# The second product of both MLPs by one level of Strassen's scheme: seven block products in place of eight

## The chip, the cores and the metric

The kernel runs on one core of one Trainium2 chip. Its metric is the device time of one execution in microseconds (us); three runs before the change gave a median of 1163.3 us (1161.93 to 1166.11). A core has TensorE (PE, matrix products; PEld is its weight load), VectorE (DVE), ScalarE (ACT), GpSimd (Pool) and SyncE (SP), whose queue issues all loads and stores here.

## The reference, cut to what matters

Two residual layers over 512 tokens of width 1024. Layer 0 mixes tokens by gating groups and stick-breaking attention, layer 1 by an mLSTM; each is followed by the same MLP with 4096 inner columns.

```python
def _sqrelu_mlp(h, w1, w2):
    return jnp.square(jax.nn.relu(h @ w1)) @ w2

def reference(x, ...):
    for layer in range(DEPTH):            # DEPTH = 2
        h = _rmsnorm(x, mix_norm_g[layer])
        ...                               # even mixer, odd mixer
        h = _rmsnorm(x, mlp_norm_g[layer])
        x = x + _sqrelu_mlp(h, mlp_w1[layer], mlp_w2[layer])
    return x
```

## The kernel before

Everything lies transposed: the residual `xs` (xres) is eight tiles of 128 features by 512 tokens. All large products are made in float32r, and each operand is split into a rounded part and the rest (`hi`, `lo`); `mm3` then makes three products, hi x hi, hi x lo and lo x hi (L228, L229, L230). The operand of the current part is `xhi`, `xlo`.

The weights come in half units of 128x1024 float32 (512 KB), in the order of their use. `w_fetch` loads one on SP's queue into `wr` (two buffers), ACT copies its rounded part to `wh` (L168) and DVE subtracts to `wl` (L169); `wh` and `wl` have six buffers each. `w_take(n)` hands out the next n units and fetches six further ones ahead (LA).

An MLP (`mlp`, called once after each mixer) runs over 8 groups of 512 inner columns. The first product of a group makes 4 tiles, each in a PSUM bank of tag A or C with 24 products of 128x512; DVE takes it out with the ReLU and the norm's factor (`r`, L561), ACT squares it (`s`, L563), ACT and DVE split it (`hh`, L224, and `hl`, L225). The second product makes the 8 feature tiles `d` one after another, each in a bank of tag B (three of them) with 12 products of 128x512, and DVE adds the bank to `xs` (L578). In the last group of the last MLP each tile is stored at once (L580), the eighth in two halves.

In the last group of the first MLP `enter` goes along: as soon as a tile of `xs` is final, ACT and DVE make the next part's `xhi` and `xlo` (L220, L221), ACT squares it (L276), and the squares are added up (L277), on Pool, the last on DVE. `norm_cols` makes the factor of each token from the sum, and the odd mixer's first values (`proj_v`) use it when their banks are taken out.

The program is written in this order and a scheduler puts each engine's instructions into the order in which they are issued; every engine then works through its own queue in order.

## Time and profile before

| | |
|---|---|
| median of 3 runs | 1163.3 us (1161.93 to 1166.11) |
| span of the profiled execution, first to last instruction | 1157.4 us |
| what lies around the span, median less span | 5.9 us |
| PE busy | 1136.7 us, 98% |
| PE weight loads | 927.1 us, 80% |
| DVE busy | 635.3 us, 55% |
| ACT busy | 448.2 us, 39% |
| Pool busy | 159.9 us, 14% |
| loads from memory | 102 MB, 26.9% of the 16 DMA engines' time |

The profiled execution has a span but no time of its own; its time is taken as the span and the 5.9 us around it. Matmuls are pipelined and their ends are modelled: a single one of 128x512 is shown as 0.39 us long while the next starts 0.23 us after it. So the distance from start to start is what a product costs, not the length of its row. Busy times of DVE and ACT can be read as they stand; back to back, their rows overlap a little.

### The profile page before, as it was taken

The page shows a single profiled execution, that of the slowest core. Times are in us where ns is not written, and L with a number is a line of the kernel's source. Part 1 is how long each engine was busy: PE and PEld are TensorE (multiplying, and loading weights), DVE is VectorE, ACT ScalarE, POOL GpSimd, SP SyncE. Part 2 cuts the span into 40 slices and gives each one's busy share as a digit, 9 for nine tenths or more (in the row PEclk, how much of TensorE's full clock was granted, in tenths as well). Part 3 has the DMA queues.
Part 4 walks back from the last instruction along what each step waited for, and adds up shares of the span by engine and source line. Part 5 has one row for each costly group of instructions (what it writes and reads, how often), then busy time and mean ns, then how long its engine had stood idle before and what let it go on. Part 6 is the DMA issues. An engine that isn't in the chain of part 4 may idle for free.

```text
span 1157.4 us, 13308 instructions
## 1 busy us (share of the span) xinstructions
PE 1136.7 (98%) x5220; PEld 927.1 (80%) x5220; DVE 635.3 (55%) x916; ACT 448.2 (39%) x704; POOL 159.9 (14%) x152
## 2 busy tenths in 40 slices
PE   8999989999999999999999999999999999999998
PEld 5788777878888888888898888887888888888886
DVE  7753698644354353453667665878452453443542
ACT  5443686542142241241555443435331331331330
POOL 7327554510000000000020010013000000000000
PEclk8999999999999999999999999999999999999999
DMA  6323210242241241331332203312231331321421
GB/s 230 106 73 110 76 35 1 92 130 73 73 146 50 96 127 55 110 114 66 113 110 73 92 26 102 110 52 94 83 117 52 112 110 52 130 99 48 146 73 73
DMA packets 33486, 105.01 MB, mean 91 GB/s; under 512 B 3600, under 2 KB 8208, under 8 KB 33424
## 3 DMA queue, kind: packets, MB, share of 16 engines
q1 hardware_dynamic: 33424, 104.17, 26.9%
q8 instruction: 41, 0.67, 0.2%
q14 instruction: 21, 0.17, 0.1%
HBM read 102.06 MB, written 2.10 MB: 90 GB/s over the span
## 4 chain that ended last, share of the span: by engine, by line
PE 90%; DVE 5%; ACT 1%; POOL 1%; DMA 1%; issue 1%; SPq 0%; DVEq 0%; ACTq 0%; POOLq 0%
PE psB L228 11%; PE psB L229 11%; PE psB L230 11%; PE psA L230 11%; PE psA L228 11%; PE psA L229 11%; PE psC L228 5%; PE psC L230 5%; PE psC L229 5%; PE psO L228 2%; PE psO L230 2%; PE psO L229 2%; DVE m L475 2%; DMA xres<-xT 1%; DVE xlo L225 0%
## 5 line engine op out<-in xcount | busy, mean ns | idle before, releaser
L168 ACT ACTIVATE wh<-wr 128x1024 fp32r<-128x1024 f32 (+1 forms) x188 | 197.7, 1060 | 456.8 <-PE psB L229 285.4
L169 DVE TENSOR_TENSOR wl<-wr,wh 128x1024 fp32r<-128x1024 f32 x172 | 214.2, 1254 | 151.1 <-ACT wh L168 145.9
L578 DVE TENSOR_TENSOR xres<-psB,xres 128x512 f32<-128x512 f32 x129 | 85.9, 684 | 249.9 <-PE psB L230 249.9
L229 PE MATMUL psB<-hl,wh 128*128 128x512 f32 x512 | 199.2, 394 | 0.0
L230 PE MATMUL psB<-hh,wl 128*128 128x512 f32 x512 | 199.0, 394 | 0.0
L228 PE MATMUL psB<-hh,wh 128*128 128x512 f32 x512 | 194.2, 394 | 0.0
L228 PEld LDWEIGHTS psB<-hh,wh 128*128 128x128 f32 x512 | 96.1, 188 | 23.1 <-DVE xres L578 0.6
L229 PE MATMUL psA<-xlo,wh 128*128 128x512 f32 x292 | 114.4, 392 | 0.0
L229 PEld LDWEIGHTS psB<-hl,wh 128*128 128x128 f32 x512 | 96.2, 188 | 22.6
L230 PEld LDWEIGHTS psB<-hh,wl 128*128 128x128 f32 x512 | 96.1, 188 | 22.5
L228 PE MATMUL psA<-xhi,wh 128*128 128x512 f32 x288 | 112.5, 392 | 0.6 <-ACT wh L168 0.6
L230 PE MATMUL psA<-xhi,wl 128*128 128x512 f32 x288 | 112.9, 392 | 0.0
L228 PE MATMUL psC<-xhi,wh 128*128 128x512 f32 x256 | 101.0, 395 | 0.0
L230 PE MATMUL psC<-xhi,wl 128*128 128x512 f32 x256 | 100.8, 394 | 0.0
L229 PE MATMUL psC<-xlo,wh 128*128 128x512 f32 x256 | 100.6, 393 | 0.0
L228 PE MATMUL psA<-wh,xhi 128*128 128x512 f32 (+2 forms) x232 | 88.5, 383 | 2.0 <-ACT wh L168 1.9
L229 PE MATMUL psA<-wl,xhi 128*128 128x512 f32 (+2 forms) x232 | 88.6, 382 | 0.9 <-DVE wl L169 0.9
L230 PE MATMUL psA<-wh,xlo 128*128 128x512 f32 (+2 forms) x232 | 88.0, 381 | 0.7 <-DVE xlo L225 0.7
L277 POOL TENSOR_TENSOR ssq<-ssq,sq 128x512 f32<-128x512 f32 x18 | 27.6, 1536 | 362.4 <-ACT sq L276 362.4
L228 PEld LDWEIGHTS psA<-xhi,wh 128*128 128x128 f32 x288 | 54.1, 188 | 13.0 <-ACT wh L168 1.0
L229 PEld LDWEIGHTS psA<-xlo,wh 128*128 128x128 f32 x292 | 54.9, 188 | 12.0
L230 PEld LDWEIGHTS psA<-xhi,wl 128*128 128x128 f32 x288 | 54.1, 188 | 11.9
(334 smaller groups left out, 1728.4 us busy)
## 6 DMA issues: line engine op xcount, KB each, us to landing
wr<-wall SPq DMA_DIRECT2D x186, 512.0 KB, 3.5
out<-xres SPq DMA_DIRECT2D x7, 256.0 KB, 2.0
wr<-wv SPq DMA_DIRECT2D x2, 528.0 KB, 4.0
xres<-xT SPq DMA_DIRECT2D x4, 256.0 KB, 6.4
xres<-xT SPq DMA_DIRECT2D x2, 512.0 KB, 9.0
lngb<-lngb SPq DMA_DIRECT2D x1, 512.0 KB, 5.5
sgr<-sgw SPq DMA_DIRECT2D x1, 512.0 KB, 6.3
out<-xres SPq DMA_DIRECT2D x2, 128.0 KB, 1.7
```

Of the source, the lines that this page charges most:

```text
L168: act.activation(hi[:, :n], raw[:, :n], AF.Copy)
L169: (gp if i in POOL_LO else dve).tensor_tensor(lo[:, :n], raw[:, :n], f(hi[:, :n]), op=ALU.subtract)
L228: pe.matmul(out, lhsT=lh, rhs=rh, start=first, stop=False)
L229: pe.matmul(out, lhsT=lh, rhs=rl, start=False, stop=False)
L230: pe.matmul(out, lhsT=ll, rhs=rh, start=False, stop=last)
L277: (dve if i == KT - 1 else gp).tensor_tensor(ssq, ssq, j, op=ALU.add)
L475: dve.tensor_tensor_scan(m[:, ::-1], m[:, ::-1], ones.to_broadcast([P, n]), 1.0, op0=ALU.mult, op1=ALU.mult)
L578: dve.tensor_tensor(xs[:, d, cq], b[:, cq], xs[:, d, cq], op=ALU.add)
```

## The change

The second product is made as 2x2 blocks by Strassen's scheme (in the variant with fifteen sums) with seven block products. The blocks split the inner columns (a group is now 1024 columns, two blocks of 512; four groups in place of eight), the output features (0 to 511 and 512 to 1023) and the tokens (two halves of 256, `H`). Half `s` of a group covers 256 features of each feature block.

- Weights: `stream` takes the place of `w_fetch`. For a half it loads the four blocks b11, b12, b22, b21 (128x1024 each, the same bytes as before) into `wq` tiles and makes four sums of them on DVE (`w_sum`, L196), into `wq` tiles too (seven buffers for both). Seven units are split on ACT (L189) and DVE (L190) in place of four. `wh` and `wl` have five buffers instead of six.
- Activations: `operands` makes from the squared tiles (`h`) the seven right-hand operands of `PROD`, four of them by differences on DVE (L644, L654), each split on ACT (L636) and DVE (L640, L638), in two portions `q` of half a group.
- Products: `prod` runs 24 products of 128x256 for a block product, two output tiles in the two halves of a bank. a11 and a12 share a bank, n3 and -a22, n1 and n4; the banks are added from PSUM to `xs` and to `accm`, a tile of 128x1024, seven times a half (L680).
- `accm` collects what four groups give to three output blocks. It is added to them (three adds of 128x512) behind the last group's half, so the four tiles of a half become final together; `enter` or the stores (L694) follow then.
- The pool `vp` of the odd mixer, with the load of `gbias` and the memsets of `v_tiles`, is opened after the first MLP instead of before it.

```diff
+NG = 4
+F_ORDER = (0, 1, 4, 5, 2, 3, 6, 7)
...
     def mlp(l):
         w1, w2 = f("mlp_w1")[l], f("mlp_w2")[l]
-        for g in range(8):
-            for ft in range(4):
-                stat_cols(w1, (4 * g + ft) * P)
-            rows(w2[g * 512:(g + 1) * 512])
+        for g in range(NG):
+            for ft in F_ORDER:
+                stat_cols(w1, (8 * g + ft) * P)
+            for s in range(2):
+                for kb, nb in ((0, 0), (0, 1), (1, 1), (1, 0)):
+                    r0, c0 = g * 1024 + kb * 512, nb * 512 + s * 256
+                    hu.append(w2[r0:r0 + 512, c0:c0 + 256].reshape(4, P, 256).transpose(1, 0, 2).reshape(P, 1024))
...
+    NRAW = 7
+    NSPL = 5
...
+    def w_sum(a, b):
+        cnt[0] += 1
+        t = q_tile(f"wq_s{cnt[0]}")
+        dve.tensor_tensor(t, a, b, op=ALU.add)
+        return t
+
+    def stream():
...
+            if m is not None and (i - m) % 16 >= 8:
+                b11 = w_load(i, True)
+                w_split(b11, i)
+                yield
+                b12 = w_load(i + 1, True)
+                b22 = w_load(i + 2, True)
+                w_split(w_sum(b12, b22), i)
+                yield
+                a = w_sum(b11, b12)
+                w_split(a, i)
+                yield
+                b21 = w_load(i + 3, True)
+                w_split(b21, i)
+                yield
+                c = w_sum(a, b22)
+                w_split(w_sum(c, b21), i)
+                yield
+                w_split(b22, i)
+                yield
+                w_split(c, i)
+                yield
+                i += 4
...
+    PROD = ("a11", "n3", "n1", "a12", "-a22", "n4", "s2")
+    H = T // 2
...
+                put("a11", a11)
+                diff("n3", a21, a11)
+                n1 = diff("n1", a21, a22)
+                put("a12", a12)
+                put("-a22", a22, True)
+                s2 = mp.tile([P, 2, H], F32, name=f"s2_{cnt[0]}", tag="ad", bufs=3)
+                dve.tensor_tensor(s2, a11, n1, op=ALU.subtract)
+                diff("n4", a12, s2)
+                put("s2", s2)
...
+                        for dd in range(2):
+                            o = bk[key][:, dd * H:(dd + 1) * H]
+                            for k in range(4):
...
+                                pe.matmul(o, lhsT=lh, rhs=rh, start=first, stop=False, skip_group_check=True)
+                                pe.matmul(o, lhsT=lh, rhs=rl, start=False, stop=False, skip_group_check=True)
+                                pe.matmul(o, lhsT=ll, rhs=rh, start=False, stop=fin, skip_group_check=True)
...
+                    add(mv, prod("a11", "a", True, False), ALU.subtract)
+                    add(blk(1, 1, s), prod("n3", "b", True, False))
+                    add(blk(1, 1, s), prod("n1", "c", True, False))
+                    add(blk(0, 0, s), prod("a12", "a", False, True))
+                    add(blk(0, 1, s), prod("-a22", "b", False, True), ALU.subtract)
+                    add(blk(1, 0, s), prod("n4", "c", False, True))
+                    add(mv, prod("s2", "d", True, True, "O"))
+                    if g == NG - 1:
+                        add(blk(1, 0, s), mv)
+                        add(blk(1, 1, s), mv)
+                        add(blk(0, 1, s), mv, ALU.subtract)
+                        for d in (2 * s, 2 * s + 1, 4 + 2 * s, 5 + 2 * s):
+                            if last:
+                                nc.sync.dma_start(out=O["out"][d], in_=xs[:, d, :])
+                            yield d
```

Where the instructions stand now. On DVE, where the first product of a group in the first MLP ends and the second begins, before the change:

```order
L561 SCALAR_TENSOR_TENSOR r_3186<-psC_3161,rrow 128x512
L169 TENSOR_TENSOR wl_3157<-wr_3155,wh_3156 128x1024
L225 TENSOR_TENSOR hl_3191<-s_3188,hh_3190 128x512
L578 TENSOR_TENSOR xres<-psB_3218,xres 128x512
L578 TENSOR_TENSOR xres<-psB_3232,xres 128x512
```

The same place on DVE in the changed kernel's second group (n_206 and s_206 are the differences n1 and s2; psB_3315 is the bank of a11, psB_3341 that of n3):

```order
L710 SCALAR_TENSOR_TENSOR r_3246<-psC_3221,rrow 128x512
L190 TENSOR_TENSOR wl_3186<-wq_s_3183,wh_3185 128x1024
L644 TENSOR_TENSOR n_206_3255<-h_3111,h_3180 128x512
L640 TENSOR_TENSOR a12l_2940<-h_3180,a12h_2939 128x512
L196 TENSOR_TENSOR wq_s_3291<-wq_3275,wq_3281 128x1024
L680 TENSOR_TENSOR accm<-accm,psB_3315 128x512
L638 SCALAR_TENSOR_TENSOR -a22l_2942<-h_3180,-a22h_2941 128x512
L654 TENSOR_TENSOR s_206_3263<-h_3111,n_206_3255 128x512
L190 TENSOR_TENSOR wl_3218<-wq_3053,wh_3217 128x1024
L640 TENSOR_TENSOR n1l_2938<-n_206_3255,n1h_2937 128x512
L680 TENSOR_TENSOR xres<-xres,psB_3341 128x2x256
```

Between the evacuation of the last first-product and the add of the first bank stood one split and one `hl`; now two splits, a sum and the first operand steps stand among the adds, and n1's second part comes tenth.

On PE at the same place, before the change (bank of the last first-product, then the first tile of the second product):

```order
L230 MATMUL psC_3161<-xhi,wl_2910 128x512
L228 MATMUL psB_3218<-hh_3073,wh_2915 128x512
L229 MATMUL psB_3218<-hl_3074,wh_2915 128x512
L230 MATMUL psB_3218<-hh_3073,wl_2916 128x512
L228 MATMUL psB_3218<-hh_3112,wh_2921 128x512
```

And on PE in the changed kernel, two block products later (a11 and n3, 24 rows each, stand ahead of this piece):

```order
L676 MATMUL psB_3341<-n3h_2935,wl_3058 128x256
L674 MATMUL psB_3367<-n1h_2937,wh_3114 128x256
L675 MATMUL psB_3367<-n1l_2938,wh_3114 128x256
L676 MATMUL psB_3367<-n1h_2937,wl_3115 128x256
L674 MATMUL psB_3367<-n1h_2937,wh_3114 128x256
L675 MATMUL psB_3367<-n1l_2938,wh_3114 128x256
L676 MATMUL psB_3367<-n1h_2937,wl_3115 128x256
L674 MATMUL psB_3367<-n1h_2937,wh_3114 128x256
L674 MATMUL psB_3315<-a12h_2939,wh_3148 128x256
L675 MATMUL psB_3315<-a12l_2940,wh_3148 128x256
```

The scheduler breaks n1 off after seven products (the first six use the older portion of its operand), runs the whole of a12 and two products of s2, and takes up n1 again behind them.

At the end of the kernel DVE's last rows were

```order
L578 TENSOR_TENSOR xres<-psB_8908,xres 128x512
L578 TENSOR_TENSOR xres<-psB_8923,xres 128x512
L578 TENSOR_TENSOR xres<-psB_8938,xres 128x256 x2
```

and are now, with all eight stores of 128x512 behind the weights' loads in SP's queue, four of them for these last three adds:

```order
L680 TENSOR_TENSOR xres<-xres,psB_10403 128x2x256
L680 TENSOR_TENSOR accm<-accm,psO_10504 128x512
L680 TENSOR_TENSOR xres<-xres,accm 128x2x256 x3
```

Where the first MLP ends, the same adds stand among the splits of the odd mixer's weights, with the second parts of its operand (L283) and the sum of squares (L339) behind them:

```order
L680 TENSOR_TENSOR accm<-accm,psO_5268 128x512
L190 TENSOR_TENSOR wl_5100<-wr_5097,wh_5099 128x1024
L680 TENSOR_TENSOR xres<-xres,accm 128x2x256 x3
L190 TENSOR_TENSOR wl_5106<-wr_5103,wh_5105 128x1024
L283 SCALAR_TENSOR_TENSOR xlo<-xres,par,xhi 128x512 x4
L339 TENSOR_TENSOR ssq<-ssq,sq_7_5314 128x512
```

Before, the adds of the tiles came one by one, each followed by its own `xlo`.

## Rows read from the trace of the kernel before

**Rows 1.** The page's table of engines: busy us, share of the span, instructions.

```profile
span 1157.4 us, 13308 instructions
PE 1136.7 (98%) x5220; PEld 927.1 (80%) x5220; DVE 635.3 (55%) x916; ACT 448.2 (39%) x704; POOL 159.9 (14%) x152
```

**Rows 2.** The page's chain that ended last, its shares of the span by engine.

```profile
PE 90%; DVE 5%; ACT 1%; POOL 1%; DMA 1%; issue 1%; SPq 0%; DVEq 0%; ACTq 0%; POOLq 0%
```

**Rows 3.** Who waited for whom, over the whole span: us in total, times, longest. The last two are PE's own waits for weights.

```profile
ACT wh L168 <- PE psB L229: 285.4, 16, 23.1
DVE wl L169 <- ACT wh L168: 145.9, 108, 10.1
...
PE psA L228 <- ACT wh L168: 2.5, 2, 1.9
...
PE psA L229 <- DVE wl L169: 0.9, 1, 0.9
```

**Rows 4.** Stretches of the span: us, then busy us (instructions) of PE, PEld, DVE, ACT, Pool, then the granted clock, the DMA share and GB/s. The first lies inside the first MLP, the second around its end.

```profile
480.00:530.00 50.00, 50.00 (x219) 40.63 (x218) 21.80 (x27) 13.15 (x16) 0.00 (x0) 1.00 0.26 86
...
580.00:630.00 50.00, 49.45 (x326) 44.10 (x324) 34.99 (x58) 28.46 (x40) 5.80 (x8) 1.00 0.32 106
```

**Rows 5.** The chain that ended last in order of time (start, us, what): the same three products in three groups that follow one another in the first MLP.

```profile
436.06 0.70 PE psB L228 x3
480.48 0.70 PE psB L228 x3
524.85 0.69 PE psB L228 x3
```

**Rows 6.** PE's instructions in order of time in the odd mixer (start, us): the first and the last of 39 products of 128x256 in a row.

```profile
604.99 0.28 PE L229 MATMUL psA<-wl,xhi 128*128 128x256 f32 x1
...
609.50 0.28 PE L228 MATMUL psA<-wh,xhi 128*128 128x256 f32 x1
```

**Rows 7.** PE's weight loads in order of time (start, us) in a run of such products: two neighbours, and the last of 18.

```profile
599.88 0.19 PEld L229 LDWEIGHTS psA<-wl,xhi 128*128 128x128 f32 x1
600.00 0.19 PEld L230 LDWEIGHTS psA<-wh,xlo 128*128 128x128 f32 x1
...
601.89 0.19 PEld L228 LDWEIGHTS psA<-wh,xhi 128*128 128x128 f32 x1
```

**Rows 8.** Groups of instructions of DVE and ACT in 330 to 580 us, inside the first MLP: busy us, mean ns of one, idle before them and its releaser.

```profile
L169 DVE TENSOR_TENSOR wl<-wr,wh 128x1024 fp32r<-128x1024 f32 x43 | 52.2, 1224 | 40.5 <-ACT wh L168 40.3
L578 DVE TENSOR_TENSOR xres<-psB,xres 128x512 f32<-128x512 f32 x46 | 30.7, 688 | 87.2 <-PE psB L230 87.2
L225 DVE TENSOR_TENSOR hl<-s,hh 128x512 fp32r<-128x512 f32 x24 | 16.6, 691 | 1.3 <-ACT hh L224 1.2
...
L168 ACT ACTIVATE wh<-wr 128x1024 fp32r<-128x1024 f32 x43 | 45.1, 1059 | 142.9 <-PE psB L229 108.2 <-DMA wr<-wall 33.5 <-PE psA L230 1.1
L224 ACT ACTIVATE hh<-s 128x512 fp32r<-128x512 f32 x23 | 14.5, 629 | 0.6
```

**Rows 9.** DVE in order of time in the first MLP (start, us of the merged row): three adds and two splits back to back.

```profile
481.91 1.89 DVE L578 TENSOR_TENSOR xres<-psB,xres 128x512 f32<-128x512 f32 x3 [3.83 <-PE psB L230]
...
499.98 2.36 DVE L169 TENSOR_TENSOR wl<-wr,wh 128x1024 fp32r<-128x1024 f32 x2 [0.86 <-ACT wh L168]
```

**Rows 10.** The page's DMA issues: count, KB each, median us from issue to landing.

```profile
wr<-wall SPq DMA_DIRECT2D x186, 512.0 KB, 3.5
out<-xres SPq DMA_DIRECT2D x7, 256.0 KB, 2.0
...
out<-xres SPq DMA_DIRECT2D x2, 128.0 KB, 1.7
```

**Rows 11.** The end of the chain that ended last in order of time: the last product and the first half of the last add.

```profile
1153.52 0.25 PE psB L230
1153.77 0.02 issue
1153.79 0.42 DVE xres L578
```

**Rows 12.** The last row of DVE in order of time, both halves merged; the span ends at 1157.4.

```profile
1153.79 0.76 DVE L578 TENSOR_TENSOR xres<-psB,xres 128x256 f32<-128x256 f32 x2 [2.10 <-PE psB L230]
```

**Rows 13.** SP's queue in order of time at the start, issues that wait for nothing.

```profile
13.32 0.43 SPq L331 DMA_DIRECT2D lngb<-lngb  x1
13.79 0.43 SPq L333 DMA_DIRECT2D sgr<-sgw  x1
```

**Rows 14.** DVE in order of time where the first MLP ends.

```profile
584.92 0.75 DVE L221 SCALAR_TENSOR_TENSOR xlo<-xres,par,xhi 128x512 fp32r<-128x512 f32 x1
...
586.18 1.72 DVE L169 TENSOR_TENSOR wl<-wr,wh 128x1024 fp32r<-128x1024 f32 x1
588.13 1.48 DVE L221 SCALAR_TENSOR_TENSOR xlo<-xres,par,xhi 128x512 fp32r<-128x512 f32 x1 [0.23 <-ACT xhi L220]
```

**Rows 15.** Pool in order of time in the same stretch and just before it.

```profile
581.47 1.34 POOL L277 TENSOR_TENSOR ssq<-ssq,sq 128x512 f32<-128x512 f32 x1 [1.45 <-ACT sq L276]
...
585.09 1.73 POOL L277 TENSOR_TENSOR ssq<-ssq,sq 128x512 f32<-128x512 f32 x1
587.56 1.50 POOL L277 TENSOR_TENSOR ssq<-ssq,sq 128x512 f32<-128x512 f32 x1 [0.74 <-ACT sq L276]
```

More of the change, by code (lines that the diff above doesn't have):

```diff
@@ L167, in w_fetch, with w_split @@
         nc.sync.dma_start(out=raw[:, :n], in_=src)
-        act.activation(hi[:, :n], raw[:, :n], AF.Copy)
-        (gp if i in POOL_LO else dve).tensor_tensor(lo[:, :n], raw[:, :n], f(hi[:, :n]), op=ALU.subtract)
-        wq.append((hi, lo))
+        return raw[:, :n]
+    def w_split(raw, i):
+        k, n = len(wq), raw.shape[1]
+        hi = wpool.tile([P, 1056], F32R, name=f"wh{k}", tag="wh", bufs=NSPL)
+        lo = wpool.tile([P, 1056], F32R, name=f"wl{k}", tag="wl", bufs=NSPL)
+        act.activation(hi[:, :n], raw, AF.Copy)
+        (gp if i in POOL_LO else dve).tensor_tensor(lo[:, :n], raw, f(hi[:, :n]), op=ALU.subtract)
+        wq.append((hi, lo))
+    def w_sum(a, b):
[4 more added lines that the diff above has]
+    def stream():
+        i = 0
+        while i < n_hu:
+            m = next((b for b in MLP0 if b <= i < b + 64), None)
+            if m is not None and (i - m) % 16 >= 8:
[20 more added lines that the diff above has]
+                i += 4
+            else:
+                w_split(w_load(i), i)
+                yield
+                i += 1
+    units = stream()
     wpos = [0]
@@ L176, in w_take @@
         wpos[0] += n
-        while len(wq) < min(n_hu, wpos[0] + la):
-            w_fetch()
+        while len(wq) < wpos[0] + la:
+            if next(units, units) is units:
+                break
         return wq[a:a + n]
@@ L585, in mlp @@
                 else:
-                    for _ in group():
+                    for _ in second(g, ops):
                         pass
+    mlp(False, 2)
     vx = ExitStack()
@@ L606, in _program @@
     v_tiles(0)
-    mlp(False, 2)
     with ExitStack() as ox:
```

101 lines of the change are left out of this document (63 added, 38 removed).

## The prediction

> **What bounds the kernel now.** I read the busy table first [rows 1]: TensorE (PE) is busy 1136.7 of 1157.4 us, VectorE (DVE) 55%, ScalarE (ACT) 39%. The reader is to see that only PE can be the bound over the whole; the chain that ended last says the same, with 90% on PE [rows 2]. Then the waits [rows 3]: ACT waited 285 us for PE to free a weight buffer and DVE 146 us behind ACT, while PE's longest sum of waits for weights was 2.5 us. Then the MLP by itself [rows 4]: in 480 to 530 us PE is busy 50.00 of 50 us at a granted clock of 1.00, DVE 21.8, ACT 13.2. So a product taken out of the MLP is time taken out, as long as DVE and ACT still deliver.
>
> The span is 1157.4 us and the median 1163.3; I work the change out on the span and carry it to the median, 5.9 us above.
>
> **The products.** A group of before has 32 x 3 products of the first kind and 32 x 3 of the second, all 128x512, and repeats every 44.37 us [rows 5]: 44.37 / 192 = 0.2311 us each. The second kind is 2 MLPs x 8 groups x 96 = 1536 products, 355.0 us. After the change it is 2 MLPs x 4 groups x 2 halves x 7 block products x 24 = 2688 products, each only 256 columns wide. What such a product costs is not half of 0.2311 by right, since each still loads its own 128x128 weights. The odd mixer has a run of them: 39 start from 604.99 to 609.50 us [rows 6], 4.51 / 38 = 0.1187 us each. 2688 x 0.1187 = 319.1 us. **Term 1: -35.9 us.** Bounds: it would be nothing if one cost 355.0 / 2688 = 0.132 us, and the row is well below; the same run in another stretch gives 0.119 (-35.1).
>
> The weight load is 0.19 us long in the rows, longer than the 0.12 us from one product to the next; but loads also start every 0.12 us there [rows 7], so they overlap. The Trainium skill (TensorE: Matmul & The Clock Gate, Part 3, The mechanism) says that a load overlaps running products only if it goes to another row group, which full 128-row loads never do. By that rule load and stream would add up, and more, narrower products would lose; the rows at both widths disagree with it here.
>
> **DVE's and ACT's new work.** Durations are those of the MLP [rows 8]: 1.22 us for a 128x1024 operation, 0.69 for 128x512; back to back they follow every 1.13 and 0.60 us [rows 9]. The new sums of weights are two-operand operations of 1024 elements on the same kinds of tiles as the split L169, so I price them as that; the differences of activations as L225; the adds from PSUM as L578. A new group (two old ones) has on DVE 22 splits and 8 sums of 1024 (30 x 1.14 = 34.2), 22 operand steps, 8 evacuations and 14 adds of 512 (44 x 0.60 = 26.4): 60.6 us against PE's 192 x 0.2311 + 336 x 0.1187 = 84.3. ACT has 22 x 1.06 + 22 x 0.63 = 37.2. On average both hide.
>
> The tight part is from the last first-product of a group to the end of the next group's first one: by the order, 44 DVE rows behind r_3246, namely 15 splits, 7 sums, 14 adds and 8 operand steps, 22 x 1.14 + 22 x 0.60 = 38.3 us, even at full durations 22 x 1.22 + 22 x 0.69 = 42.0, against 336 x 0.1187 + 24 x 0.2311 = 45.4 us of PE. It fits.
>
> Whether it fits in order: let 0 be the end of w1's last product. Head of ACT's queue is wh_3185, which waits until then for its buffer, 0.2 to 1.2; the square behind it ends at 1.9. DVE: evacuation r_3246 to 0.9, split 2.4, n1's difference 3.0, a12l 3.6, the sum 4.8, accm 5.4 (its product ended at 2.9), -a22l 6.1, s2 6.7, split 7.8, n1l 8.4. PE meanwhile: a11 to 2.85, n3 to 5.7, seven products of n1 to 6.5, a12 to 9.4, two of s2 to 9.6; only then does it need n1l's second part. 1.2 us are spare, and 0.2 with every operation at full length. The next need, s2l, is ready at 11.4 for 14.5. So **term 2: 0 us per group**; from both sides, no gain is possible there (PE was never waiting), and 2 us per group if a sum or a transfer is late (16 in all). Raw weights are the same 512 KB loads, landing in 3.5 us [rows 10], into seven slots shared with the sums; carried on in the same way, the walk leaves the tightest of them (the next group's last raw tile) about 2 us between landing and its sum. I cost the loads at nothing on that cover; a tile that is later than this is the 2 us per group above.
>
> **The ends of the MLPs.** Before, the residual's last tile alone was left after the last product. Now the last bank (s2) must be added into accm, then three adds make four tiles final. At the end of the kernel that was 0.76 us of adds and 2.85 us more to the end [rows 11, 12]. Now 0.69 + 3 x 0.60 = 2.5 us of adds, four stores in a row on SP's queue, issued every 0.47 us [rows 13], which puts the last one 1.4 us later, and 256 KB land in 2.0 against 1.7 us [rows 10]: 2.5 - 0.76 + 1.4 + 0.3. **Term 3: +3.4 us** (2.5 to 5).
>
> After the first MLP the odd mixer's values need all eight xhi/xlo tiles. In DVE's order a split stands between the adds and one behind them: the third add ends at 0.69 + 1.14 + 1.8 = 3.7 us after the last product, xhi of tile 2 at 4.4, and xlo of tile 7 behind ACT's xhi and squares at about 7.8. PE has until then only some 44 products of 0.12, 5.3 us. Pool's sums of squares, which made a DVE operation 1.48 instead of 0.75 us long [rows 14, 15], lie in the same stretch. PE idled 0.55 us there before [rows 4]. **Term 4: +3 us** (2 to 7, the upper end if the norm's chain, three Pool adds of 1.34 to 1.73 us one after another [rows 15], holds the banks too).
>
> **Five split buffers for six.** In the mixers a chunk holds four weight units, so only one unit of the next is split ahead instead of two; a buffer frees 5.5 us before its next user, against 1.06 + 1.22 of splitting. Only 3.4 us of PE's waits were for weights at all [rows 3]. **Term 5: +1 us** (-1 to 5, for the scheduler also reordered these parts).
>
> Sum: -35.9 + 0 + 3.4 + 3 + 1 = -28.5 us, span 1129, median 1163.3 - 28.5 = 1134.8. I say **1135 us**.
>
> **Rivals.** (a) The queue order bites: DVE or ACT stands at the head of its queue on a buffer, a transfer or an accumulator, and PE loses 1 to 2.5 us in each of the eight groups. For it: the spare 1.2 us above, and raw tiles and sums sharing seven slots. Against: everything else has 2 us or more. It gives 1143 to 1155.
> (b) DVE becomes the bound in the second products: slower. The place is the 44 rows above. The price: if its operations ran as beside Pool (1.72 for a 1024 split, [rows 14]), 22 x 1.72 + 22 x 0.69 = 53.0 us against 45.4, 7.6 us in each of 8 groups, +61: 1196. It turns the sign from 45.4 + 28.5 / 8 = 49 us on, 28% above 38.3. Against: Pool has nothing to do inside the MLP.
> (c) The narrow product is no cheaper per column in long runs: at 0.129 us each (355.0 less the 7.4 us of the other terms, over 2688) the change does nothing, 1163. For it: the run in the rows is 4.5 us long, the new ones 40 us.
> (d) Loads bind: no product faster than its load of 0.19 us [rows 7]: 2688 x 0.19 = 511, 156 more than 355.0, and 7 of the other terms: 1326. The rows at 0.1187 speak against it. The rule of the Trainium skill cited above (same title and section) is the case for it.
>
> **Chances.** Forecast (1129 to 1143) 0.60; (a) 0.19; (c) 0.06; (b) 0.10; (d) 0.02; better than all terms 0.03. Range 1129 to 1155, which holds the first two. A measurement here tells 0.3% (3.5 us) from no change. Faster 0.82, same 0.06, slower 0.12.
>
> **What would show it.** Right: psB products 128x256 starting every 0.119 us with PE busy without gaps inside the MLPs, a group every 84.4 us, DVE near 70% there, PE idle of 3 us where the first MLP ends and about 7 us from the last product to the end of the span. Wrong: waits of PE on n1l, s2l, n4l or wl of L190 or on an add of L680, of 1 us and more in every group (a); DVE without idle time in the second products (b); products further apart than 0.12 us with no wait named (c, d).

## The result, and the profile after

The changed kernel takes 1146.8 us (median of 4 runs, 1144.97 to 1148.43) against 1162.8 for the kernel before beside it: ratio 0.9861, 95% interval 0.9842 to 0.9881, or 14 to 18 us saved. The forecast was 1135 us in a range of 1129 to 1155. So the sign and the range held, but a little over half of the 28.5 us came. The profiled execution has a span of 1143.1 us, 14.3 less than before, and that difference is accounted for here. It is not quite the difference of the medians (16.0), because the two profiled executions are not equally typical. The 5.9 us that were set around the span before are not what lies around it: the profiled execution of the changed kernel took 1144.97 us, 1.9 more than its span, so the one before was some 4 us quicker than its median, and the one after 1.8.

The page after: span, table of engines, and the chain's shares by engine, which answer to [rows 1] and [rows 2].

```profile
span 1143.1 us, 15880 instructions
PE 1107.3 (97%) x6372; PEld 960.7 (84%) x6372; DVE 829.3 (73%) x1135; ACT 525.6 (46%) x800; POOL 159.2 (14%) x154
...
PE 83%; DVE 9%; DMA 2%; POOL 2%; ACT 2%; issue 1%; SPq 0%; DVEq 0%; ACTq 0%; POOLq 0%
```

PE lost 29 us of busy time, twice what the span lost, and its share of the chain fell from 90% to 83%: something now waits that did not wait before. To find the place I cut the span at four marks that both kernels have, the products that add up a norm's squares (eight short products into psC): at the start of the even mixer, ahead of the first MLP, ahead of the odd mixer, ahead of the second MLP. First the kernel before, then the kernel after, both from the chain in order of time (start, us, what).

```profile
69.68 0.87 PE psC L382 x8
238.91 1.02 PE psC L204 x8
593.71 0.79 PE psC L204 x8
808.54 0.79 PE psC L204 x8
```

```profile
69.03 0.87 PE psC L444 x8
242.08 1.04 PE psC L266 x8
590.30 0.79 PE psC L266 x8
807.47 1.05 PE psC L266 x8
```

The last product of each MLP splits its stretch once more. First before, then after, from PE's instructions in order of time (start, us).

```profile
584.57 0.39 PE L230 MATMUL psB<-hh,wl 128*128 128x512 f32 x1
...
1153.35 0.40 PE L230 MATMUL psB<-hh,wl 128*128 128x512 f32 x1
```

```profile
571.00 0.29 PE L676 MATMUL psO<-s2h,wl 128*128 128x256 f32 x1
...
1135.81 0.28 PE L676 MATMUL psO<-s2h,wl 128*128 128x256 f32 x1
```

| stretch | before | after | difference | predicted |
|---|---|---|---|---|
| to the first MLP's norm | 238.9 | 242.1 | +3.2 | term 5: +1, for both mixers |
| first MLP, to its last product | 345.7 | 328.9 | -16.7 | term 1: -18 |
| from there to the odd mixer's norm | 9.1 | 19.3 | +10.2 | term 4: +3 |
| odd mixer | 214.8 | 217.2 | +2.3 | in term 5 |
| second MLP, to its last product | 344.8 | 328.3 | -16.5 | term 1: -18 |
| from there to the end | 4.1 | 7.3 | +3.2 | term 3: +3.4 |
| span | 1157.4 | 1143.1 | -14.3 | -28.5 |

The first 69 us are the same code, but differ from profile to profile (69.0 to 73.9 us in those of this study); so stretches are compared below, not ends. The even mixer alone, from the first mark to the second, took 169.2 us before and 173.05 after.

**Inside the MLPs** the prediction held closely. Three evacuations of DVE in order of time (start, us): the last of the first products in one group, then the first and the last in the next.

```profile
277.77 0.69 DVE L710 SCALAR_TENSOR_TENSOR r<-psC,rrow 128x512 f32<-128x512 f32 x1 [1.79 <-PE psC L292]
...
323.31 0.69 DVE L710 SCALAR_TENSOR_TENSOR r<-psA,rrow 128x512 f32<-128x512 f32 x1 [2.17 <-PE psA L292]
...
362.30 0.69 DVE L710 SCALAR_TENSOR_TENSOR r<-psC,rrow 128x512 f32<-128x512 f32 x1 [2.20 <-PE psC L292]
```

A group repeats every 362.30 - 277.77 = 84.53 us (predicted 84.3), and the stretch of the second products is 45.54 (predicted 45.4). Busy times in just that stretch (PE, PEld, DVE, ACT, Pool; granted clock, DMA share, GB/s), which answers to [rows 4]:

```profile
277.77:323.31 45.54, 45.54 (x361) 44.44 (x360) 39.49 (x46) 19.03 (x21) 0.00 (x0) 1.00 0.34 107
```

PE has no idle time; DVE has 39.5 us of work where 38.3 were counted. And 360 weight loads start in 45.54 us, one every 0.127 us, though one is 0.19 us long [rows 7]: loads overlap here in a run ten times as long as the one in [rows 6]. The rule that was weighed in the prediction comes from a list in the Trainium skill (TensorE: Matmul & The Clock Gate, Part 3, The mechanism), and it does not describe these full-row loads. The same section also says that a load can be pulled ahead of running products into a background weight buffer; the prediction left that sentence out, and it is the one that fits these rows.

**Where the first MLP ends** is the large loss. PE's waits between 560 and 605 us (us in total, times, longest):

```profile
PE psA L290 <- ACT xhi L282: 4.9, 1, 4.9
PE psO L290 <- DVE accm L680: 1.4, 1, 1.4
PE psA L292 <- DVE xlo L283: 0.7, 1, 0.7
...
```

ACT, then DVE, in order of time there (start, us; in brackets the idle time before and its releaser):

```profile
571.20 1.06 ACT L189 ACTIVATE wh<-wr 128x1024 fp32r<-128x1024 f32 x1 [6.95 <-PE psO L675]
...
577.16 1.06 ACT L189 ACTIVATE wh<-wr 128x1024 fp32r<-128x1024 f32 x1 [3.42 <-DVE xres L680]
578.12 1.93 ACT L282 ACTIVATE xhi<-xres,par 128x512 fp32r<-128x512 f32 x3
```

```profile
572.29 1.22 DVE L190 TENSOR_TENSOR wl<-wr,wh 128x1024 fp32r<-128x1024 f32 x1 [1.12 <-ACT wh L189]
573.43 0.68 DVE L680 TENSOR_TENSOR accm<-accm,psO 128x512 f32<-128x512 f32 x1
574.03 1.22 DVE L190 TENSOR_TENSOR wl<-wr,wh 128x1024 fp32r<-128x1024 f32 x1
575.17 1.89 DVE L680 TENSOR_TENSOR xres<-xres,accm 128x512 f32<-128x512 f32 x3
...
579.39 3.76 DVE L283 SCALAR_TENSOR_TENSOR xlo<-xres,par,xhi 128x512 fp32r<-128x512 f32 x4
```

Read it as two queues whose heads wait. The bank with s2's product was complete at about 571.2, but the add that takes it into accm stood behind a split of an odd mixer's weight; that split waited for ACT's copy, and the copy for the buffer that s2's product freed at 571.2. So the add came at 573.43, and the third add ended at 577.06. ACT meanwhile stood at the copy of another weight until 577.16, with the three xhi behind it. The profile names xres as the releaser, but the copy does not read xres, and a load fits better: the split that ended at 573.5 freed one of the two raw buffers, SP's queue issued a load right then, and 573.5 + 3.5 us of loading [rows 10] is 577.0.

```profile
573.54 0.33 SPq L182 DMA_DIRECT2D wr<-wall  x1
```

PE's last wait and the last sum of squares, in order of time (start, us):

```profile
582.54 0.59 PE L292 MATMUL psA<-wh,xlo 128*128 128x264 f32 x1 [0.75 <-DVE xlo L283]
```

```profile
587.00 0.69 DVE L339 TENSOR_TENSOR ssq<-ssq,sq 128x512 f32<-128x512 f32 x1 [3.85 <-ACT sq L338]
```

From 582.54 PE works without a wait up to the norm's products at 590.30, while the sum of squares that these need is complete at 587.69. So what ends last here is PE's own products of the values behind the late xlo, and not the norm's chain. Of the 72 products of the values that stand between the last product of the MLP and the norm, PE had made 18 when it came to wait for xhi and 24 when it came to wait for xlo, and 20 of them started 0.22 us apart instead of 0.12.

### The profile page after: what moved, and what is told of

The parts are those of the page before. It is cut to its first block, busy times and chain, and to the rows that moved or that the text cites. A ratio compares the mean times of both kernels' runs of the same rounds, so it can differ in the third digit from the quotient of the medians.

```text
span 1143.1 us, 15880 instructions
## 1 busy us (share of the span) xinstructions
PE 1107.3 (97%) x6372; PEld 960.7 (84%) x6372; DVE 829.3 (73%) x1135; ACT 525.6 (46%) x800; POOL 159.2 (14%) x154
## 4 chain that ended last, share of the span: by engine, by line
PE 83%; DVE 9%; DMA 2%; POOL 2%; ACT 2%; issue 1%; SPq 0%; DVEq 0%; ACTq 0%; POOLq 0%
PE psA L292 10%; PE psA L290 10%; PE psA L291 10%; PE psB L676 8%; PE psB L674 8%; PE psB L675 8%; PE psC L292 5%; PE psC L291 5%; PE psC L290 5%; DVE m L537 2%; PE psO L290 2%; PE psO L291 2%; PE psO L292 2%; PE psO L675 1%; PE psO L674 1%
## 5 line engine op out<-in xcount | busy, mean ns | idle before, releaser
L189 ACT ACTIVATE wh<-wr 128x1024 fp32r<-128x1024 f32 (+1 forms) x124 | 131.3, 1061 | 193.8 <-DMA wr<-wall 65.2
L190 DVE TENSOR_TENSOR wl<-wr,wh 128x1024 fp32r<-128x1024 f32 (+1 forms) x108 | 137.0, 1273 | 58.0 <-ACT wh L189 57.6
L189 ACT ACTIVATE wh<-wq_s 128x1024 fp32r<-128x1024 f32 x64 | 67.9, 1061 | 121.6 <-PE psB L675 64.2
L189 ACT ACTIVATE wh<-wq 128x1024 fp32r<-128x1024 f32 x48 | 51.0, 1062 | 77.1 <-PE psB L675 24.5
L190 DVE TENSOR_TENSOR wl<-wq_s,wh 128x1024 fp32r<-128x1024 f32 x64 | 78.0, 1219 | 4.2 <-ACT wh L189 4.2
L710 DVE SCALAR_TENSOR_TENSOR r<-psC,rrow 128x512 f32<-128x512 f32 x32 | 22.1, 690 | 74.1 <-PE psC L292 74.1
L339 POOL TENSOR_TENSOR ssq<-ssq,sq 128x512 f32<-128x512 f32 x18 | 27.5, 1530 | 345.7 <-ACT sq L338 345.7
L680 DVE TENSOR_TENSOR xres<-xres,psB 128x512 f32<-128x512 f32 x80 | 53.9, 680 | 23.9 <-PE psB L676 23.9
L292 PEld LDWEIGHTS psA<-xhi,wl 128*128 128x128 f32 x288 | 54.1, 188 | 12.2 <-DVE wl L190 0.8
L190 DVE TENSOR_TENSOR wl<-wq,wh 128x1024 fp32r<-128x1024 f32 x48 | 58.5, 1219 | 2.3 <-ACT wh L189 2.3
L290 PEld LDWEIGHTS psC<-xhi,wh 128*128 128x128 f32 x256 | 48.7, 190 | 11.3
```

What stands on the lines that cost most here:

```text
L189: act.activation(hi[:, :n], raw, AF.Copy)
L190: (gp if i in POOL_LO else dve).tensor_tensor(lo[:, :n], raw, f(hi[:, :n]), op=ALU.subtract)
L290: pe.matmul(out, lhsT=lh, rhs=rh, start=first, stop=False)
L292: pe.matmul(out, lhsT=ll, rhs=rh, start=False, stop=last)
L339: (dve if i == KT - 1 else gp).tensor_tensor(ssq, ssq, j, op=ALU.add)
L680: add = lambda dst, b, op=ALU.add: dve.tensor_tensor(dst, dst, b, op=op)
```

## The experiments

**Is the narrow product really cheap?** The kernel before, with each 128x512 product of the second kind cut into two of 128x256 (3072 instead of 1536).

```
- for ft in range(4): mm3(b, ..., hs[ft][0], hs[ft][1], ...)
+ for e in range(2):
+     cq = slice(e * 256, (e + 1) * 256)
+     for ft in range(4): three products of 256 columns into b[:, cq]
```

> The kernel before with the second product of both MLPs in 3072 products of 128x256 instead of 1536 of 128x512, each with its own weight load; all eight block products stay, and no sums. Theory (a narrow product costs 0.1187 to 0.119 us in long runs too): 3072 x 0.1188 = 365 for 355, +10 us, 1173. Rival (the narrow product is dearer in long runs, 0.129): 396 for 355, +41 us, 1204. Rival (the load of 0.19 binds): 584 for 355, +229 us.

Measured: 1173.25 us, ratio 1.0093 (1.0070 to 1.0115), +10.8 us. (355.0 + 10.8) / 3072 = 0.1191 us a product over stretches of 23 us. Rivals (c) and (d) fall; the halved width costs 3%, not 12%.

**The five split buffers.** The kernel before, with five buffers for wh and wl in place of six.

```
- tag="wh", bufs=6        - tag="wl", bufs=6
+ tag="wh", bufs=5        + tag="wl", bufs=5
```

> The kernel before with five wh and wl buffers instead of six, nothing else. Theory (the mixers lose what the change takes from the split buffers): the changed kernel came to the first MLP's norm 3.2 us later than before (242.1 for 238.9) and needed 2.5 us more for the odd mixer, so about +5.7 us here, 1168, with the loss before 240 us and between 594 and 809 us of the span, and under 1 us in the MLPs. Rival (the mixers lose from other things: the pool vp moved, another order by the scheduler): 0 to +1 us, 1163.

Measured: 1168.8 us, ratio 1.0045 (1.0027 to 1.0063), +5.2 us by the ratio. Term 5 was priced at +1. In its profile the even mixer takes 171.3 us (+2.1) and the odd one 216.2 (+1.4); the second MLP is 2.2 us longer too, against an expected loss of under 1 us there. Then the other way round: the changed kernel with six split buffers, and six raw slots to make room.

```
- NRAW = 7        - NSPL = 5
+ NRAW = 6        + NSPL = 6
```

> The changed kernel with six buffers for split weights, as the kernel before has, and six instead of seven slots for raw tiles and their sums. Theory (term 5 was mis-sized, the five buffers cost the mixers about 5 us, as the kernel before with five buffers lost 5 to 6): 1141 to 1142 (ratio 0.982). Rivals: six raw slots are too few and TensorE waits for a split weight in the second products, 1 to 2 us in each group: 1150 to 1158; or the five buffers cost nothing in this kernel and the time stays 1146.8 (0.986).

Measured: 1143.2 us, ratio 0.9826 (0.9804 to 0.9847), against 0.9861 for the changed kernel: 3.6 us back, near what was expected, though the two intervals still touch. Its first two marks in the chain:

```profile
72.20 0.87 PE psC L444 x8
241.82 1.04 PE psC L266 x8
```

The even mixer between them is 169.6 us; it was 169.2 before and 173.05 after. The buffer is only half of that loss. PE's granted clock falls once in the even mixer, and in the profiles of this study it does so at one of two places, whatever the number of buffers:

| split buffers | clock low, us behind the first mark | even mixer, us | profiles |
|---|---|---|---|
| six | 70 to 76 | 169.2 to 169.6 | before, e2_narrow, e8_nspl66, e12_early66 |
| six | 80 to 84 | 171.1 | e11_all |
| five | 70 to 76 | 171.2 to 171.4 | e1_before_5buf, e4_sums2, e5_fill, e7_rawq, e10_rawq_bias, e13_sums3 |
| five | 80 to 84 | 172.9 to 173.05 | after, e3_early, e6_early_rawq |

At the same place, 80 to 84 us behind the mark, in the changed kernel and then in e1_before_5buf (busy us and instructions, clock third from the end):

```profile
149.03:153.03 4.00, 4.00 (x16) 3.27 (x17) 3.51 (x7) 2.43 (x6) 1.68 (x4) 0.57 0.01 5
```

```profile
153.47:157.47 4.00, 4.00 (x26) 3.19 (x27) 4.00 (x9) 3.41 (x10) 1.68 (x4) 1.00 0.00 1
```

So in the even mixer the fifth buffer less costs 1.9 us, and the place where the clock falls another 1.6. What decides that place is not shown. Of the odd mixer's 2.3 us the sixth buffer gives 1.0 back; the rest stays open.

**How far is DVE from being the bound?** The changed kernel with every sum of two weights made twice, and in a second kernel three times.

```
  dve.tensor_tensor(t, a, b, op=ALU.add)
+ dve.tensor_tensor(t, a, b, op=ALU.add)      (two of these in e13_sums3)
```

> The changed kernel in which every sum of two weight tiles is made twice into the same tile: 8 more VectorE operations of 128x1024 in each of the 8 groups (64 x 1.13 = 72 us of VectorE work), nothing else. It measures how far VectorE is from being the bound in the second products, which is the point from which rival (b) decides. By the walk of the prediction, the stretch holds 38.3 us of VectorE work against 45.4 us of TensorE; with 7 sums doubled it is 46.2, 0.8 us over, so TensorE should lose about 1 to 3 us in each of 8 groups: +8 to +20 us against the changed kernel (ratio to the kernel before 0.993 to 1.003). If VectorE still has room (its work is shorter than the rows make it), the time stays within 3 us of the changed kernel's 1146.8. If VectorE already sets the pace there, all 72 us show: about 1218 (ratio 1.048).

> The changed kernel with every sum of two weight tiles made three times: 16 more VectorE operations of 128x1024 in each of the 8 groups than the changed kernel, 8 more than e4_sums2. In e4_sums2's trace the stretch between the two evacuations that bound the second products of a group had VectorE busy 46.72 of 46.72 us and TensorE 45.71, and nothing was lost over the run; so the bound should lie there. With 7 sums more in the stretch it is 46.7 + 7 x 1.13 = 54.6 us, against 45.5 us of TensorE: 7 to 9 us lost in each of 8 groups, 1204 to 1220 (ratio 1.035 to 1.05). Rival: VectorE's surplus is carried into the first products behind, where it has 16 us spare (23.07 busy of 38.99 in the changed kernel), and only little is lost: 1150 to 1165.

Measured: twice, 1148.46 us, ratio 0.9876 (0.9849 to 0.9904), no loss that can be told from the changed kernel's 0.9861. Three times, 1214.8 us, ratio 1.0450 (1.0418 to 1.0481), +68 us, 8.5 in a group on average. The stretch from a group's last evacuation to the next group's first, for the first two groups of the first MLP, with the sums made twice, then three times:

```profile
279.16:325.88 46.72, 45.71 (x358) 44.13 (x357) 46.72 (x54) 17.40 (x21) 0.00 (x0) 1.00 0.30 91
364.56:410.60 46.04, 46.04 (x364) 44.88 (x363) 43.66 (x49) 17.43 (x20) 0.00 (x0) 1.00 0.27 85
```

```profile
278.86:338.19 59.33, 51.53 (x353) 48.14 (x353) 57.09 (x63) 18.57 (x21) 0.00 (x0) 0.91 0.27 82
376.97:430.09 53.12, 49.30 (x361) 47.44 (x360) 49.66 (x56) 17.89 (x21) 0.00 (x0) 0.94 0.28 82
```

With the sums made twice DVE has no idle time at all in the first of these stretches, 46.72 of 46.72 us, and PE still loses only 1.0 us of it. From the second group on DVE has 2.4 us to spare and only four more instructions in the stretch than the changed kernel (49 for 45), so some of the extra work has moved into the first products behind; a group repeats every 84.57 us there, 84.53 in the changed kernel. Made three times, the stretch takes 59.3 us in the first group and 53.1 and 52.1 in the next two, and PE's longest wait, 4.3 us, names ACT, which copies the sums that DVE delivers late. So rival (b) turns the time somewhere between 8 and 16 further sums in a group, near the lower end, since of the last 64 sums, 72 us at 1.13, 66 us were paid.

The 1 to 3 us a group that were expected of a surplus of 0.8 us did not come. The rival of the second kernel, that a larger surplus is carried into the first products and little is lost, failed.

**The end of the first MLP: late accumulator.** The changed kernel, with s2's product second in the last half of each MLP (a11, s2, n3, ...), so that accm is final early and n4's add comes last. The stream of weights follows that order.

```
+ PROD_L = ("a11", "s2", "n3", "n1", "a12", "-a22", "n4")
+ early = g == NG - 1 and s == 1
- ws = dict(zip(PROD, w_take(7)))
+ ws = dict(zip(PROD_L if early else PROD, w_take(7)))
```

> The changed kernel with another order in the last half of each MLP's last group alone: s2 is made second instead of last, accm is added to the three blocks early, and the last product (n4) leaves one add and two tiles. The weights' sums and splits of that half follow in the new order. Theory (the ends of the MLPs lose because accm's adds come last): at the end of the kernel 1.8 us of adds and 0.9 of stores go, about -2.9; at the end of the first MLP, where 72 products took 19.0 us for 8.7, about -8. Together -11 us against the changed kernel, 1136, ratio to before 0.977. Rival (the stall at the first MLP's end is due to the weights' loads and the norm's chain, which stay): -3 us, 1144.

Measured: 1142.55 us, ratio 0.9823 (0.9803 to 0.9843), 4.3 us less than the changed kernel and not the 11 that were expected. That is nearer to the rival's 1144. From the start of the last product to the end of the span it was 4.9 instead of 7.3 us, the stretch from the MLP's norm to the odd mixer's 344.3 instead of 348.2. The distance from the first MLP's last product to the norm says nothing here: it is 9.1 us, but 18 products of the values now stand ahead of that product, and the product itself comes 6.3 us later behind the MLP's norm. ACT still stood at its queue's head:

```profile
575.40 1.06 ACT L189 ACTIVATE wh<-wr 128x1024 fp32r<-128x1024 f32 x1 [7.64 <-DMA wr<-wall]
```

Here the profile names the load: with a second wait of 2.65 us it is 10.3 us of ACT's waiting for raw weights, with xhi at 580.07 behind them.

**The clock.** In the changed kernel PE's idle time is followed by a lower clock. Stretches of the changed kernel:

```profile
575.00:580.00 5.00, 0.17 (x2) 0.00 (x0) 3.81 (x6) 2.84 (x5) 1.13 (x9) 0.59 0.65 209
580.00:585.00 5.00, 4.15 (x17) 3.84 (x18) 3.15 (x4) 2.45 (x5) 2.89 (x2) 0.50 0.38 105
```

To price that, 48 products without use were put behind the last product of the first MLP; they only add work.

```
+ b = bank("B")
+ for _ in range(48):
+     pe.matmul(b[:, :256], lhsT=ops["n3"][0][:, 0, :P], rhs=ops["a11"][0][:, 0, :], start=True, stop=True)
```

> The changed kernel with 48 more products of 128x256 behind the last product of the first MLP, into a bank that nobody reads, so that TensorE isn't idle for the 5 us in which it waits for xhi. Theory (part of the stall's price is the granted clock, which fell from 1.00 to 0.50 there and stood at it until 586 us, so that 38 products took 0.22 instead of 0.12 us each): the clock stays at 1.00, and what the 48 products take (5.7 us) lies in the idle time; -3.7 us against the changed kernel, 1143. Rival (the clock costs nothing, the chain of adds, xhi and squares sets the end): 0. If the 48 products delay the real ones: +1 to +2.

Measured: 1146.2 us, ratio 0.9857 (0.9837 to 0.9877), nothing that can be told from the changed kernel's 0.9861; an effect of 2 us would not stand out of these intervals either. The first of the same stretches of that kernel, and PE's last wait in it:

```profile
575.00:580.00 5.00, 5.00 (x42) 4.82 (x40) 3.87 (x6) 1.86 (x3) 1.14 (x9) 1.00 0.73 210
```

```profile
583.52 0.39 PE L292 MATMUL psA<-wh,xlo 128*128 128x264 f32 x1 [1.43 <-DVE xlo L283]
```

The trace tells more than the time. The clock stayed at 1.00. From PE's last wait to the norm it takes 6.2 us (583.52 to 589.68), 7.8 in the changed kernel (582.54 to 590.30), and from the last product of the MLP to the norm 17.9 instead of 19.3. So the lower clock costs about 1.5 us at this place. That is less than the 3.7 of the expectation, which counted 38 products at 0.22 us: the trace has 20, and 16 of them lie behind the last wait. The gain does not show from norm to norm, 348.0 us against 348.2, since in this profile the first MLP began at a lower clock (0.60 from 244 to 248 us, 1.00 at that place in the changed kernel) and had lost 1.2 us before its second products.

**The raw weights.** Four raw tiles of the odd mixer go into the MLP's slots instead of the two raw buffers, so that they land before the first MLP ends; alone, then together with e3_early's order.

```
- w_split(w_load(i), i)
+ w_split(w_load(i, V0 + 2 <= i < V0 + 6), i)
```

> The changed kernel with one thing else: the raw tiles of four weight units of the odd mixer (the third to the sixth) are loaded into the seven slots that the MLP's raw tiles use, not into the two raw buffers that a unit's VectorE split has to free first. So they can be in the chip before the first MLP ends. Theory: ScalarE's queue at the end of the first MLP is held up by weight copies whose raw tiles have not landed, and the copies of the normed activations wait behind them. Then TensorE's idle stretch before the values (about 4.9 + 1.4 + 0.7 us there) shrinks by 3 to 4 us: 1143 to 1144 (ratio 0.983), and ScalarE waits for no load at 571 to 578 us. Rival: the late third add into the accumulator alone sets the stretch, then the time is the changed kernel's, 1146.8 (0.986).

> Both edits: the product with s2 put second in the last half of each MLP (as in e3_early, measured at 0.982 of the kernel before), and the four raw tiles of the odd mixer in the MLP's slots (as in e7_rawq). Theory: in e3_early ScalarE still waited 7.6 and 2.7 us for raw loads where the first MLP ends; with these gone the boundary costs some 5 to 6 us less than in e3_early: about 1137 (ratio 0.977). Rival: the norm's chain (copies, squares on GpSimd, sums, row of factors) is then what ends last, and no more than 2 us come: 1140.5 to 1142.5 (0.981 to 0.982).

Measured: alone 1148.69 us, ratio 0.9872 (0.9848 to 0.9896), no gain; with the order 1143.35, ratio 0.9826 (0.9804 to 0.9849), no gain over e3_early. The trace of e7_rawq shows that the place was right: ACT waits for no load there, and the stretch from the MLP's norm to the odd mixer's is 344.55 us, 3.6 less. DVE's last xlo and PE's last wait at the end of its first MLP, whose last product starts at 573.85:

```profile
578.86 3.75 DVE L283 SCALAR_TENSOR_TENSOR xlo<-xres,par,xhi 128x512 fp32r<-128x512 f32 x4
```

```profile
582.00 0.59 PE L292 MATMUL psA<-wh,xlo 128*128 128x264 f32 x1 [1.08 <-DVE xlo L283]
```

The last xlo ends 8.8 us behind the last product there, 12.2 in the changed kernel, and the norm comes after 16.1 us instead of 19.3.

But the odd mixer took 221.3 instead of 217.2. PE waits 2.5 us for the transposes of the gates and has a granted clock of 0.66 in 595 to 600 us (1.00 in the changed kernel). DVE's row there, and the wait of SP's queue before the issue of the gates' biases (us in total, times, longest), in e7_rawq:

```profile
596.35 0.36 DVE L769 SCALAR_TENSOR_TENSOR gpre<-psA,rc,gbias 128x8 f32<-128x8 f32 x2 [0.26 <-DMA gbias<-gbias]
```

```profile
SPq L724 <- DVE wl L190: 22.8, 1, 22.8
```

and the same wait in the changed kernel:

```profile
SPq L724 <- DVE xres L680: 1.4, 1, 1.4
```

DVE's operation waited for the biases, though only 0.26 us; it also stood behind two splits, the last of which ended at 596.09. PE's transposes need what it makes. The load of 4 KB was issued at 594.7 us instead of 577.2. I read that as a place behind the weight loads in SP's queue. So it was moved to the start of the kernel:

```
+ gbias = const.tile([P, 8], F32, name="gbias")       (loaded with the constants)
- gbias = vpool.tile([P, 8], F32, name="gbias")
```

> e7_rawq with the 4 KB load of the gates' biases (gbias) moved to the start of the kernel; nothing else. In e7_rawq's trace the stretch from the MLP's first norm product to the odd mixer's was 3.6 us shorter than in the changed kernel, and the stretch from there to the second MLP's 4.1 us longer. Theory: the gain was given back because SP's queue issued gbias only at 594.7 us (577.2 in the changed kernel), behind a weight load that waited for its slot, so that the gates' first VectorE operation came late and TensorE waited 2.5 us for it, and then ran at half clock. With gbias early the odd mixer is as long as in the changed kernel, 217 us, and 3.5 to 4 us come back: 1144.5 to 1145.5 (ratio 0.984). Rival: the odd mixer is longer for another reason (its steps were reordered with the loads), then the time stays 1148.7 (0.987).

Measured: 1146.6 us, ratio 0.9861 (0.9838 to 0.9885). 2.1 us less than e7_rawq, not told apart by the intervals; the odd mixer is 219.9 us, so 1.4 of the 4.1 us came back. The waits above show what that reading overlooked: the issue waited for the split of a raw tile that sits in the MLP's slots, not for a load. The odd mixer's pool is opened after the MLP's, and by these waits its tiles wait until the MLP's last slot is free. In the changed kernel that is the end of the third add, 577.06, in e7_rawq the split that ends at 594.64, in e6_early_rawq one that ends at 591.54 (its gbias was issued at 591.61, and its odd mixer took 224.0 us). Moving gbias leaves the other tiles of that pool where they were: in e10_rawq_bias Pool's first memset into it starts at 592.44, released by the same split, for 577.16 in the changed kernel, gpre still stands behind that split, PE waits 0.9 and 0.8 us at the transposes, and its granted clock is 0.67 in 595 to 600 us. Raw tiles in the MLP's slots gained nothing.

**Together.** e3_early's order, six split buffers and gbias early (e12_early66), and the same with the raw tiles in the MLP's slots (e11_all).

```
+ PROD_L = ("a11", "s2", "n3", "n1", "a12", "-a22", "n4")   (e3_early)
+ NRAW = 6
+ NSPL = 6
+ gbias loaded with the constants
+ w_split(w_load(i, V0 + 2 <= i < V0 + 6), i)               (e11_all only)
```

> All four edits on the changed kernel: s2's product second in the last half of each MLP (e3_early), four raw tiles of the odd mixer in the MLP's slots (e7_rawq), six buffers for split weights with six raw slots (e8_nspl66), and gbias loaded at the start. If the gains add up: 4.3 of the first, some 4 of the buffers and 1 to 2 of the loads, about 1137 (ratio 0.977). Rival: with six raw slots the odd mixer's early tiles take slots that the last half of the first MLP needs, TensorE waits for a weight there, and e12_early66 without them is faster: 1140 (0.980).

> e11_all without the raw tiles in the MLP's slots: s2's product second in the last half of each MLP, six buffers for split weights with six raw slots, gbias early. If these gains add up, 1142.55 - 3.6 = 1139 (ratio 0.979); the difference to e11_all then is what the raw tiles are worth where no other load is held up by them, 1 to 2 us by the theory, nothing by the rival.

Measured: e11_all 1136.1 us, ratio 0.9769 (0.9746 to 0.9792); e12_early66 1132.4 us, ratio 0.9736 (0.9713 to 0.9759), 30 us less than the kernel before and 14 less than the changed one. It beats both; the raw tiles in the MLP's slots cost 3.7 us here by the medians, whose intervals overlap (344.4 us between the norms of e11_all, 340.8 of e12_early66; 1.1 of these 3.6 us are lost at the start of the first MLP, ahead of the tiles). The marks of e12_early66 from its chain:

```profile
69.87 0.87 PE psC L466 x8
239.44 1.04 PE psC L287 x8
580.24 1.05 PE psC L287 x8
796.59 1.05 PE psC L287 x8
```

ACT's waiting for raw weights between 555 and 582 us, 10.3 us in e3_early and 10.0 in e8_nspl66, is 1.5 us here. From mark to mark, in us:

| stretch | before | after | e3_early | e8_nspl66 | e12_early66 |
|---|---|---|---|---|---|
| even mixer | 169.2 | 173.05 | 172.9 | 169.6 | 169.6 |
| first MLP's norm to the odd mixer's | 354.8 | 348.2 | 344.3 | 345.7 | 340.8 |
| odd mixer | 214.8 | 217.2 | 217.5 | 216.2 | 216.4 |
| second MLP's norm to the end | 348.9 | 335.6 | 334.8 | 335.8 | 331.5 |

Between the norms of the first MLP 10.1 of the 16.7 us that its products save were lost again in the changed kernel; in e12_early66 it is 2.7. Neither edit alone clears that place: e8_nspl66 still takes 18.2 us from its last product to the norm, since its accumulator is last, and e3_early's weights are late. By the medians the gains of e3_early (4.3) and e8_nspl66 (3.6) add to 8, and 14 came. Behind the first mark the profiled executions gain 4.6, 6.8 and 15.8 us, so 4.4 more than the sum. About 1 us of that lies at the first MLP and 3.4 in the last stretch, where the clock is most of the difference: at the start of the second MLP it falls in e3_early and e8_nspl66, and their first products take 1.3 to 1.5 us longer there, while in e12_early66 and the changed kernel it stays at 1.00 behind an equally short idle of 1.3 us. In e3_early, 2 us behind the norm:

```profile
809.33:811.33 2.00, 2.00 (x6) 1.55 (x5) 1.42 (x3) 0.00 (x0) 1.64 (x1) 0.50 0.36 47
```

Early gbias was not run by itself on these kernels, so its share is not shown.

## Why the prediction was right in sign and wrong in size

- **Term 1, the products (-35.9): right.** -16.7 and -16.5 us in the two MLPs, -33.2. A group takes 84.53 us for 84.25, (84.53 - 44.37) / 336 = 0.1195 us a product instead of 0.1187, which is 2 of the 2.7 us that are missing.
- **Term 2, nothing per group: right.** No wait on n1l, s2l or a weight comes back in each group; PE is 45.54 of 45.54 us busy. The hand walk of DVE's queue erred by 1.2 us in 38.3, and in e4_sums2 7 us more in a stretch still cost nothing that can be measured. The spare 1.2 us on which rival (a) rested were no edge.
- **Term 3, the end (+3.4): right.** +3.2. The adds and the stores, from the last rows of DVE and of SP's queue in the kernel after; by the page a store lands 2.3 us after its issue:

```profile
1136.12 0.69 DVE L680 TENSOR_TENSOR accm<-accm,psO 128x512 f32<-128x512 f32 x1 [2.06 <-PE psO L676]
1136.84 1.90 DVE L680 TENSOR_TENSOR xres<-xres,accm 128x512 f32<-128x512 f32 x3
```

```profile
1138.16 1.79 SPq L694 DMA_DIRECT2D out<-xres  x4
```

- **Term 4, the end of the first MLP (+3, bound 7): wrong, +10.2.** Three things failed.
  The first is the step "the third add ends at 3.7 us after the last product, xhi of tile 2 at 4.4, and xlo of tile 7 at about 7.8". They came at 6.1, 7.8 and 12.2. The walk let each queue run as if its head were always ready. It named the split between the adds, but not that the split ahead of accm's add waits for ACT's copy, the copy for a buffer that s2's product frees, and the next copy for a raw tile whose buffer that split frees. In e7_rawq, where these copies were done early, the last xlo came at 8.8, near the walk, and the place cost 3.2 us less.
  The second is the overlap, "PE has until then only some 44 products of 0.12": it had 24, 18 of them before xhi, and the 20 that were missing are 2.4 us.
  The third has no term in the sum: the lower clock behind PE's idle time, about 1.5 us by e5_fill. These two are why e7_rawq, with the walk nearly right, still loses 6.9 us there and not 3.
  With the +3 of the sum the 3.2, the 2.4 and the 1.5 make some 10. The norm's chain that gave the upper bound does not end last here, as it is ready 2.6 us before PE comes to it. It does in e3_early and e12_early66, where PE waits 1.0 us for it.
- **Term 5, five split buffers (+1, bound 5): too small.** e1_before_5buf measured +5.2 (3.1 to 7.3), e8_nspl66 got 3.6 back. The step that failed compared one buffer's 5.5 us of lead with 2.3 us of splitting. The traces place 1.9 us in the even mixer and 1.0 to 1.4 in the odd one. How a missing buffer costs that is not shown: PE's waits for a split weight in the even mixer of the changed kernel come to 0.5 us. The waits of [rows 3] priced weights at 3.4 us with six buffers and say nothing of five. Another 1.6 us of the even mixer's loss is the place where the clock fell, which the prediction had no term for.
- The rivals: (c) and (d) are refuted by e2_narrow and the traces; (b) needs more than 8 further sums in a group; (a) as it was stated did not happen, since no group lost anything. Its mechanism, a queue whose head waits for a buffer and a transfer, acted once, at the boundary. The measured 1146.8 us lies outside the forecast's 1129 to 1143 and inside the stated range only by the part that was added for (a), so that it is inside is partly luck.

## What to carry to other kernels

A saving on the engine that sets the pace is read well from spacings of the same shape elsewhere in the trace. The ends of stages are not read from durations: follow there, for each queue, what its head waits for (a buffer, whose release is another queue's step, whose input is a load), and count the load's time into the chain. Count too which products the engine can really make before its wait, in the order in which it takes its operands. A prefetch buffer given up for space, and tiles of the next stage put into the slots of this one, are paid in other stages than the one that is changed, so they are best run by themselves. And before a difference of 1 to 2 us between two profiles is put down to an edit, compare the granted clock of the same stretch in both.

## What the runs showed of the hardware that was not expected

- DVE busy without a gap in one group's second products, 46.72 of 46.72 us, cost the run nothing measurable. 64 more operations of 1.13 us then cost 66 of their 72 us.
- PE's granted clock was 0.59 in the 5 us in which it was nearly idle and 0.50, the lower of its two levels, in the next 5, in which it was 83% busy, with products 0.22 us apart instead of 0.12. Keeping it at 1.00 by filler products made that place 1.4 us shorter, too little to show in the run's time.
- The clock does not fall at the same places in each profile of the same code: 70 to 76 or 80 to 84 us into the even mixer (1.6 us of difference), and at the start of an MLP in some profiles and not in others (1.2 to 1.5 us).
- SP's queue stood 22.8 us at one load of 4 KB whose tile's space was still held by a raw tile of the stage before.
